# Both row parts of the dense u side in one matmul, with a VectorE add, in a hybrid decoder trunk

## Chip, cores and metric

The kernel runs on one core of one Trainium2 chip. The metric is the device time in microseconds (us) of one execution of the whole program; several executions are timed and the median is given. Further executions were recorded by the hardware profiler.

## The reference

One decoder layer for 256 tokens of width 1024: a mixer of two attention kinds with a residual, then a layer of retrieved experts (PEER) with a residual, then a last norm. Only the expert layer is touched:

```python
q = (hf @ wq).reshape(T, PEER_HEADS, 2, PEER_QDIM // 2)          # 256 tokens, 8 heads, 2 halves
s = jnp.einsum('thpd,hpnd->thpn', q, subkeys)                    # 128 keys for each half
s1, i1 = lax.top_k(s[:, :, 0], PEER_TOPK); s2, i2 = lax.top_k(s[:, :, 1], PEER_TOPK)   # 16 each
cand = s1[..., :, None] + s2[..., None, :]                       # 16 x 16 sums
top_s, pos = lax.top_k(cand, PEER_TOPK); idx = take_along_axis(cand_idx, pos)
w = jax.nn.softmax(top_s)
act = gelu(einsum('cd,chkd->chk', x_c, u[idx_c]))                # 16384 experts, rows of u
out = einsum('chk,chkd->cd', w_c * act, v[idx_c])                # rows of v
```

All data are float32.

## The kernel before

**Two ways for the experts.** 32 of the tokens (NG) read the rows of u and v that they chose: gathers by index bring 128 rows at a time to SBUF, VectorE takes 32 dot products with u rows (`dot`) and 32 weighted sums of v rows (`row_sum`). The other 224 tokens (TD) are computed against all 16384 experts: gelu(u·x) for every expert and token is made densely, multiplied by weights that one-hot matmuls spread over the experts, and multiplied with v.

**Two parts of each number.** A float32 product is made of rounded parts: `whi` is the weight rounded by ScalarE (`high`), `wlo` the rest, by VectorE (`low`); `ah` and `al` are the two parts of the tokens' rows. A block is one matrix of 128 experts by 1024. `block_t` runs 24 matmuls of 224 columns for it: ah with whi and al with whi in turn over 8 chunks, then ah with wlo, all into one region of PSUM.

**Stages.** Projections and attention; peer_wq (the queries, 16 blocks); u, first half (64 blocks, in pairs e = 0 to 31); u, second half (64 blocks), with the one-hot products beside it; v (128 blocks); and a tail that adds, transposes, norms and writes.

**Order.** `slot` issues one block: the load of a block two or three ahead (`fetch`, SyncE's queue, three raw buffers), then what stands in `first`, whi of the block two ahead, its wlo, what was put into `late`, what stands in `pre`, and last the block's matmuls. whi and wlo have three buffers each as well. In PSUM the names pj, pT, pS and pO have two banks each.

**Beside the matmuls of the first half** the top-16 search, the softmax and the look-up of the indices run. They are a list of steps, each with a price in us; `advance(us)` adds to a credit and runs the steps that it pays for. In the first half each slot adds PACE. The steps: 16 picks over rows of keys for each of the two token halves b (most on VectorE), `cands`, four picks `best`, `decode` (shifts and five casts), `soft_exp`, `choose`, then for both sets k = 0, 1: `look_idx`, `look_eq`, `look_tab`, `look_mul`, `look_sum` and `look_end` (four sums that halve a 128x2048 bf16 tile down to 128x128). `route` sends the 32 tokens' indices to memory and back as gather indices; `tables(b)` transposes weights and indices for the one-hot products. `tokens_out` lays the 32 tokens' rows out for the gathers by a GpSimd transfer.

A pair's end in the first half is one line, gelu read from PSUM by ScalarE (L1229):

```python
nc.scalar.activation(g, pu, AF.Gelu)
```

Of the kernel before, what the change touches and what calls it, by code (L numbers as in the profile page):

```python
# [141 lines left out]
def body(tc, nc, a):  # L142
# [849 lines left out]
    def decode(b):  # L992
        def it(name, dt=U32):
            return sel.tile([P, 8, 16], dt, name=name)
        pos = cp[b]
        hi4, lo4, hi2, lo2 = it("hi4"), it("lo4"), it("hi2"), it("lo2")
        nc.vector.tensor_scalar(hi4, pos, 4, None, OP.logical_shift_right)
        nc.vector.tensor_scalar(lo4, pos, 15, None, OP.bitwise_and)
        nc.vector.tensor_scalar(hi2, pos, 2, None, OP.logical_shift_right)
        nc.vector.tensor_scalar(lo2, pos, 3, None, OP.bitwise_and)  # L1000
        f = [it(f"f{k}", F32) for k in range(5)]
        for k, s in enumerate((hi4, lo4, hi2, lo2, pos)):
            nc.vector.tensor_copy(f[k], s)
        fs[b] = f
# [23 lines left out]
    def look_idx(b, k):  # L1028
        tib[b, k] = sel.tile([P, 8, 16], BF, name="tib", bufs=2)
        nc.vector.tensor_copy(tib[b, k], ti[b][:, :, k])  # L1030

# [11 lines left out]
    def look_sum(b, k):  # L1043
        e = eq[k]
        for n in (8, 4):
            nc.vector.tensor_tensor(e[:, :, 0:n], e[:, :, 0:n], e[:, :, n:2 * n], OP.add)
# [69 lines left out]
    for b in range(2):  # L1116
        steps.append((1.2, cands, b))
        for m in range(4):
            steps += pick(best, b, m)
            if b == 1 and m == 0:  # L1120
                steps.append((0.5, tables, 0))
        steps += [(0.3, soft_sub, b), (1.2, decode, b), (0.1, soft_exp, b), (1.2, choose, b), (0.2, look_idx, b, 0),
                  (1.15, look_eq, b, 0), (0.0, look_tab, b, 0), (0.7, soft_div, b), (0.2, look_idx, b, 1),
                  (1.15, look_mul, b, 0),
                  (1.15, look_eq, b, 1), (0.0, look_tab, b, 1), (0.95, look_sum, b, 0), (0.6, look_end, b, 0), (1.15, look_mul, b, 1),
                  (0.95, look_sum, b, 1), (0.6, look_end, b, 1)]
        if b == 0:
            steps.append((0.3, route))
    first_dot = next(k for k, v in enumerate(steps) if v[1:] == (soft_sub, 1))
    front, behind = steps[:first_dot], steps[first_dot:]  # L1130
    share, done, n = sum(v[0] for v in behind) / DOTS[0], 0.0, 0
    for v in behind:
        front.append(v)
        done += v[0]
        while n < DOTS[0] and done >= share * (n + 0.5):
            front.append((1.35, dot, n))
            n += 1
    steps = front + [(0.5, tables, 1)]
    credit = [0.0]
# [67 lines left out]
    def u_pair(e, first=((), ()), pre=((), ())):  # L1207
        box = []

        def use(hi, lo):  # L1210
# [20 lines left out]

        slot(use, first[0], pre[0])
        slot(use, first[1], pre[1])
        late.append(evac)

    for e in range(32):
        pre = ((rows_out,), (io_tables,)) if e == 0 else ((lambda: score(7),), ()) if e == 1 else ((), ())
        if e == 4:
# [152 lines left out]
    def fold_in():  # L1391
        nc.gpsimd.dma_start(xq[1].rearrange("p (g d) -> p g d", g=NR),
                            ys.rearrange("(g t) (c d) -> (t c) g d", t=NG, c=NR))

    def fold():
        n = D // 2
        while n >= D // NR:
            nc.gpsimd.tensor_tensor(xq[1][:, :n], xq[1][:, :n], xq[1][:, n:2 * n], OP.add)
# [40 lines left out]
    n += 3 + 5 * (NG - 1) // 2  # L1439
    at_slot(n + 2, "v", fold_in)  # L1440
# [31 lines left out]
    def turn_rows(c):  # L1472
        for b in range(2):
            nc.tensor.transpose(turned[c // 4 * 2 + b][:TB, (c % 4) * P:(c % 4 + 1) * P],
                                lasts[c][:, b * TB:(b + 1) * TB], ident)
# [7 lines left out]
    def total(b, c0, c1, n):  # L1483
        d = c0 // 4
        cs = slice((c0 - 4 * d) * P, (c1 - 4 * d) * P)
        nc.scalar.activation(whole[:, cs], turned[2 * d + b][:TB, cs], AF.Square, scale=1.0 / 32.0,
                             accum_out=sq[b][:, n:n + 1])
# [60 lines left out]
```

## Time and profile before

| what | value |
|---|---|
| median of 3 runs | 983.03 us (982.72 to 983.94) |
| profiled execution | 983.31 us; its span 981.5 us |
| busy in the span | TensorE 968.4, VectorE 801.7, ScalarE 587.7, GpSimd 141.2 us |
| u side, first half | 275.0 to 448.1 us |
| u side, second half | 448.1 to 646.7 us |
| v side | 646.7 to 957.3 us |

The span is the recorded stretch from first to last instruction; the execution's time has some 1.8 us more around it. PE is TensorE, PEld its weight loads, DVE VectorE, ACT ScalarE, POOL GpSimd, SP SyncE. A row of a group gives line, engine, operation, output and inputs, their shapes, the count, then busy time and mean duration in ns, then the engine's idle time before and what ended it. A row of the timeline gives start, duration and the instruction, in square brackets its engine's idle time before it and what ended that. A row of the windows gives start:end, length, busy time of each engine with its count of instructions, the granted clock of TensorE, the share of DMA time and GB/s. A row of the chain gives start, length, engine, output and line.

### The profile page before, as it was taken

The numbers are of one execution on the slowest core, as the hardware profiler recorded it, in microseconds if no ns is written. First come the engines' busy times: TensorE is split into PE (matmuls) and PEld (weight loads), VectorE is DVE, ScalarE is ACT, GpSimd is POOL, SyncE is SP. The second block draws the span as 40 slices with busy tenths as digits, with TensorE's granted clock in tenths as the row PEclk, the third lists the DMA queues.
The fourth block names the chain that finished last, engine by engine and source line by source line (L and its number), as shares of the span: only waits on it lengthen the run. The fifth ranks groups of instructions, "written<-read, shape, count | busy, mean of one in ns | idle before, by whom it ended". The sixth has DMA issues, their size and how long they took to land.

```text
span 981.5 us, 20223 instructions
## 1 busy us (share of the span) xinstructions
PE 968.4 (99%) x7825; PEld 938.0 (96%) x7825; DVE 801.7 (82%) x1486; ACT 587.7 (60%) x1073; POOL 141.2 (14%) x113
## 2 busy tenths in 40 slices
PE   9999999999999999999999999999999999999995
PEld 7898999999999999999999999999999999999995
DVE  5788876877889998887989999878778888888766
ACT  7545544656555665556988888655555555555563
POOL 3000110000000011321001001013313333333100
PEclk9999999999999999999999999999999999999999
DMA  8723434566556667887656655678878888787771
GB/s 274 264 90 111 124 114 132 173 195 188 176 174 219 220 200 253 309 277 265 204 194 198 211 183 183 215 262 291 294 271 299 296 287 293 287 293 292 274 224 44
DMA packets 61424, 217.24 MB, mean 221 GB/s; under 512 B 7120, under 2 KB 8320, under 8 KB 61320
## 3 DMA queue, kind: packets, MB, share of 16 engines
q1 hardware_dynamic: 48352, 174.42, 54.0%
q0 software_dynamic: 11280, 39.68, 11.0%
q10 hardware_dynamic: 1696, 1.84, 0.6%
q8 instruction: 62, 1.02, 0.4%
q14 instruction: 34, 0.28, 0.1%
HBM read 212.86 MB, written 2.52 MB: 219 GB/s over the span
## 4 chain that ended last, share of the span: by engine, by line
PE 91%; DVE 5%; ACT 1%; DMA 1%; issue 1%; SPq 0%; DVEq 0%; ACTq 0%
PE pj L372 50%; PE acc L1351 21%; PE acc L1355 11%; PE pw L1298 3%; DVE wlo L204 1%; PE pS L665 1%; PE pS L504 1%; PE pT L637 1%; PE pS L1166 1%; DMA xg<-in_x 1%; DMA raw<-in_w_t 1%; ACT whi L200 0%; PE pO L648 0%; PE pO L649 0%; PE pj L769 0%
## 5 line engine op out<-in xcount | busy, mean ns | idle before, releaser
L204 DVE TENSOR_TENSOR wlo<-raw,whi 128x1024 fp32r<-128x1024 f32 (+2 forms) x329 | 398.9, 1213 | 100.1 <-ACT whi L200 99.2
L200 ACT ACTIVATE whi<-raw 128x1024 fp32r<-128x1024 f32 (+2 forms) x329 | 343.7, 1045 | 138.1 <-PE pj L372 51.7
L372 PE MATMUL pj<-ah,whi 128*128 128x224 f32 (+1 forms) x1344 | 320.0, 282 | 0.2
L372 PE MATMUL pj<-al,whi 128*128 128x224 f32 (+1 forms) x1344 | 314.0, 276 | 0.6 <-DVE al L332 0.4
L372 PEld LDWEIGHTS pj<-al,whi 128*128 128x128 f32 x1344 | 257.5, 192 | 2.2 <-DVE al L332 1.0
L372 PEld LDWEIGHTS pj<-ah,whi 128*128 128x128 f32 x1344 | 256.7, 191 | 2.1 <-issue 1.2
L1351 PE MATMUL acc<-co,whi 128*128 128x448 f32 x1024 | 231.1, 367 | 0.1
L1351 PEld LDWEIGHTS acc<-co,whi 128*128 128x128 f32 x1024 | 182.8, 189 | 11.8 <-issue 0.3
L372 PE MATMUL pj<-ah,wlo 128*128 128x224 f32 (+1 forms) x1344 | 180.8, 276 | 0.0
L372 PEld LDWEIGHTS pj<-ah,wlo 128*128 128x128 f32 x1344 | 165.9, 191 | 0.0
L1355 PEld LDWEIGHTS acc<-co,wlo 128*128 128x128 f32 x1024 | 134.8, 191 | 4.2 <-DVE wlo L204 0.8
L1355 PE MATMUL acc<-co,wlo 128*128 128x224 f32 x1024 | 135.1, 273 | 0.5 <-DVE wlo L204 0.5
L1262 ACT ACTIVATE co<-G 128x224 fp32r<-128x224 f32 x128 | 50.1, 392 | 142.1 <-PE acc L1355 142.1
L1091 POOL DMA_INDIRECT row<-in_v_n,sidx x32 | 62.2, 1944 | 146.4 <-DVE ysum L1386 125.2
L1286 ACT ACTIVATE onehot<-onehot,wl 128x128 f16<-128x128 f16 x224 | 71.3, 392 | 6.3 <-DVE onehot L1290 5.9
L1263 DVE TENSOR_TENSOR co<-G,co 128x224 fp32r<-128x224 f32 x128 | 50.4, 394 | 22.2 <-ACT co L1262 21.9
L1091 POOL DMA_INDIRECT row<-in_u_n,sidx x19 | 32.8, 1729 | 218.0 <-DVE row L1101 217.4
L372 PE MATMUL pj<-bh,whi 128*128 128x256 f32 x192 | 48.0, 286 | 0.0
L372 PE MATMUL pj<-bl,whi 128*128 128x256 f32 x192 | 47.4, 284 | 0.0
L1386 DVE SCALAR_TENSOR_TENSOR ysum<-row,acts,ysum 128x1024 f32<-128x1024 f32 x31 | 39.7, 1280 | 0.0
L632 ACT ACTIVATE prob<-pS,nm 128x128 f32<-128x128 f32 (+1 forms) x48 | 19.8, 416 | 30.6 <-DVE nm L629 30.6
L372 PEld LDWEIGHTS pj<-bl,whi 128*128 128x128 f32 x192 | 36.5, 190 | 0.0
(323 smaller groups left out, 929.5 us busy)
## 6 DMA issues: line engine op xcount, KB each, us to landing
raw<-in_u_t SPq DMA_DIRECT2D x128, 512.0 KB, 3.5
raw<-in_v_n SPq DMA_DIRECT2D x128, 512.0 KB, 4.3
raw<-in_w_m SPq DMA_DIRECT2D x16, 512.0 KB, 3.5
raw<-in_w_q SPq DMA_DIRECT2D x16, 512.0 KB, 3.7
raw<-in_w_t SPq DMA_DIRECT2D x15, 512.0 KB, 5.0
raw<-in_w_b SPq DMA_DIRECT2D x8, 512.0 KB, 3.5
raw<-in_w_o SPq DMA_DIRECT2D x8, 512.0 KB, 3.6
sg<-in_w SPq DMA_DIRECT2D x4, 512.0 KB, 6.4
```

What stands on the lines that cost most here:

```text
L200: return [lambda s=slice(u, min(v, n)): nc.scalar.activation(hi[:, s], raws[k][:, s], AF.Copy) for u, v in cuts]
L204: nc.vector.tensor_tensor(lo[:, cs], raws[k][:, cs], hi[:, cs].bitcast(F32), OP.subtract)
L372: nc.tensor.matmul(out, (wl if v == 2 else wh)[:, c], (l if v == 1 else h)[:, c], start=(i == 0), stop=(i == len(seq) - 1))
L632: nc.scalar.activation(p[:, o], src[b], AF.Exp, bias=nm[:, b:b + 1], accum_out=sums[:, b, h:h + 1])
L1091: nc.gpsimd.indirect_dma_start(rows_of_step(n), None, src, bass.IndirectOffsetOnAxis(ap=sidx[:, n % NG:n % NG + 1], axis=0))
L1262: nc.scalar.activation(t[:, :TD], g, AF.Copy)
L1263: nc.vector.tensor_tensor(t[:, TD:], g, t[:, :TD].bitcast(F32), OP.subtract)
L1286: nc.scalar.activation(E[:, 1, t], E[:, 1, t], AF.Copy, scale=wl[:, n:n + 1])
L1298: nc.tensor.matmul(pw[:, t * P:(t + 1) * P], E[:, 0, t], E[:, 2 - s, t], start=(s == 0), stop=(s == 1))
L1351: nc.tensor.matmul(acc[c][:, :2 * TD], w[0][:, c * P:(c + 1) * P], coefs[k], start=(k == 0), stop=False, skip_group_check=True)
L1355: nc.tensor.matmul(acc[c][:, small], w[1][:, c * P:(c + 1) * P], coefs[k][:, :TD], start=False, stop=(k == P - 1), skip_group_check=True)
L1386: nc.vector.scalar_tensor_tensor(ysum, t, w, ysum, OP.mult, OP.add)
```

## The change

In the first 30 of the 32 pairs (WIDE), `use_both` takes the place of `block_t`: ah and al become two slices of one tile `both`, so that one matmul of 448 columns multiplies whi with both parts; al's product lands in the lower half's neighbour, and wlo with ah (224 columns) is added to that upper half. That is 8 matmuls of 448 columns and 8 of 224 a block, each block in a bank of its own (pj for a pair's first block, pT for its second). `evac_both` ends a pair: ScalarE copies the two upper halves to SBUF (`lowsum`), VectorE adds the lower ones one slot later, ScalarE takes the gelu in place a slot after that.

```diff
-PACE = 1.29
+PACE = 0.92
-DOTS = (13, 22)
-FETCH = 18
+DOTS = 12
+WIDE = 30
...
-    ah = hx.tile([P, NC, T], F32R, name="ah")
-    al = hx.tile([P, NC, T], F32R, name="al")
+    both = hx.tile([P, NC, 2, T], F32R, name="both")
+    ah, al = both[:, :, 0], both[:, :, 1]
...
+        def use_both(hi, lo):
+            o = bank("pT" if box else "pj")
+            box.append(o)
+            wh, wl = (v.rearrange("p (c m) -> p c m", m=P) for v in (hi, lo))
+            for c in range(NC):
+                nc.tensor.matmul(o[:, :2 * TD], wh[:, c], both[:, c, :, NG:], start=(c == 0), stop=False,
+                                 skip_group_check=True)
+            for c in range(NC):
+                nc.tensor.matmul(o[:, TD:2 * TD], wl[:, c], ah[:, c, NG:], start=False, stop=(c == NC - 1),
+                                 skip_group_check=True)
+
+        def evac_both():
+            g = G[e // 32][:, 2 * (e % 32):2 * (e % 32) + 2]
+            t = sel.tile([P, 2, TD], F32, name="lowsum", bufs=2)
+            for j in range(2):
+                nc.scalar.activation(t[:, j], box[j][:, TD:2 * TD], AF.Copy)
+            def add():
+                for j in range(2):
+                    nc.vector.tensor_tensor(g[:, j], t[:, j], box[j][:, :TD], OP.add)
+                late.append(lambda: nc.scalar.activation(g, g, AF.Gelu))
+            late.append(add)
+            spots["blocks"] += 2
```

The work beside it moves. The five casts of `decode` and the cast of `look_idx` go from VectorE to ScalarE, the four sums of each look-up set from VectorE to GpSimd. `route` and `tables(0)` come later in the list, `tables(1)` leaves it and stands at the last pair. The dots leave the first half (13 there before): 12 stand in the second half (before 9), 20 in the v side (before 10), and there dots and row sums stand every second block instead of every 2.5. The row buffers of the first half go, and one of the two loads of the 32 tokens' rows (`tokens_in`) with them.

```diff
         for k, s in enumerate((hi4, lo4, hi2, lo2, pos)):
-            nc.vector.tensor_copy(f[k], s)
+            nc.scalar.activation(f[k], s, AF.Copy)
...
         for n in (8, 4):
-            nc.vector.tensor_tensor(e[:, :, 0:n], e[:, :, 0:n], e[:, :, n:2 * n], OP.add)
+            nc.gpsimd.tensor_tensor(e[:, :, 0:n], e[:, :, 0:n], e[:, :, n:2 * n], OP.add)
...
+        if e == 31:
+            pre = (), (lambda: tables(1),)
...
     for k in range(2):
-        at_slot(3 + 2 * k, "pre", rows_in, DOTS[0] + k)
-    for n in range(*DOTS):
-        at_slot(9 + 6 * (n - DOTS[0]), "pre", dot, n)
+        at_slot(3 + 2 * k, "pre", rows_in, k)
+    for n in range(DOTS):
+        at_slot(9 + 9 * n // 2, "pre", dot, n)
...
-    for n in range(DOTS[1], NG):
-        at_slot(1 + 5 * (n - DOTS[1]) // 2, "v", dot, n)
+    for n in range(DOTS, NG):
+        at_slot(1 + 2 * (n - DOTS), "v", dot, n)
...
-        at_slot(n + 3 + 5 * k // 2, "v", row_sum, k)
+        at_slot(n + 3 + 2 * k, "v", row_sum, k)
```

Smaller edits: in peer_wq three pairs advance by 1.6 and 1.4 instead of 1.3 and 1.2; in the tail chunk 7's transposes get two banks of their own, and the last multiplication by the norm is split in two to follow that (384 and 128 columns).

VectorE, in the first half at blocks 4 and 5. Before (sc holds the scores, tv and ti the values and indices found; wlo_3690 is of block 6, wlo_3728 of block 7):

```order
L204 TENSOR_TENSOR wlo_3690<-raw_3641,whi_3689 128x1024 [waits DMAHW6_49,PE_49,Activation_49]
L947 MATCH_REPLACE sc_2783<-tv1_2806,sc_2783 128x128 [waits DVE_49] x2
L949 MAX tv1_2806<-sc_2783 128x8 [waits DVE_49] x2
L951 MAX_INDEX ti1_2808<-tv1_2806,sc_2783 128x8 [waits DVE_49] x2
L204 TENSOR_TENSOR wlo_3728<-raw_3677,whi_3727 128x1024 [waits DMAHW7_49,PE_49,Activation_49]
```

After, at the same place (wlo_3658 is of block 6, wlo_3689 of block 7, pj_3605 and pT_3632 the banks of pair 1):

```order
L204 TENSOR_TENSOR wlo_3658<-raw_3622,whi_3657 128x1024 [waits DMAHW6_49,PE_49,Activation_49]
L939 MAX tv1_2804<-sc_2782 128x8 x2
L941 MAX_INDEX ti1_2806<-tv1_2804,sc_2782 128x8 [waits DVE_49] x2
L204 TENSOR_TENSOR wlo_3689<-raw_3649,whi_3688 128x1024 [waits DMAHW7_49,PE_49,Activation_49]
L1221 TENSOR_TENSOR G0_2781<-lowsum_3662,pj_3605 128x224
L1221 TENSOR_TENSOR G0_2781<-lowsum_3662,pT_3632 128x224
```

The adds of pair 1 now stand behind wlo of block 7. On TensorE block 6 (pair 3) takes the banks that pair 1 had, and its first matmul carries a wait for VectorE:

```order
L1207 MATMUL pj_3727<-both_137,whi_3657 128x448 [waits DVE_49,PE_49,Activation_49]
L1207 MATMUL pj_3727<-both_137,whi_3657 128x448 x7
L1210 MATMUL pj_3727<-both_137,wlo_3658 128x224 x8
L1207 MATMUL pT_3756<-both_137,whi_3688 128x448 [waits DVE_49,Activation_49]
L1207 MATMUL pT_3756<-both_137,whi_3688 128x448 x7
L1210 MATMUL pT_3756<-both_137,wlo_3689 128x224 x8
```

In the order before, block 6's first matmul waits for ScalarE alone, and its rows alternate between ah and al.

ScalarE, at the second decode and softmax (f0 to f4 are the casts, wsm the weights). Before:

```order
L983 ACT_TABLE_LOAD [waits DMASW2_49]
L983 ACTIVATE wsm_5029<-wsm_5029 128x128 [waits DVE_49]
L200 ACTIVATE whi_5149<-raw_5110 128x1024 [waits DMAHW5_49,DVE_49,PE_49]
L200 ACTIVATE whi_5189<-raw_5144 128x1024 [waits DMAHW6_49,DVE_49,PE_49]
L1229 ACT_TABLE_LOAD
L1229 ACTIVATE G0_2782<-pj_5119 128x448 [waits PE_49]
L200 ACTIVATE whi_5225<-raw_5177 128x1024 [waits DMAHW7_49,DVE_49,PE_49]
```

After (lowsum is the copy of the upper halves):

```order
L1001 ACTIVATE f3_5143<-lo2_5135 128x128 [waits DVE_49]
L1001 ACTIVATE f4_5144<-cp1_2810 128x128
L981 ACT_TABLE_LOAD
L981 ACTIVATE wsm_5105<-wsm_5105 128x128 [waits DMASW1_49]
L200 ACTIVATE whi_5151<-raw_5097 128x1024 [waits DMAHW6_49,PE_49,Activation_49]
L1222 ACT_TABLE_LOAD
L1222 ACTIVATE G0_2781<-G0_2781 128x448
L1217 ACTIVATE lowsum_5156<-pj_5080 128x224
L1217 ACTIVATE lowsum_5156<-pT_5113 128x224 [waits PE_49]
L200 ACTIVATE whi_5188<-raw_5130 128x1024 [waits DMAHW7_49,PE_49,Activation_49]
```

Casts and copies have joined the exp and the two table loads, and the copies stand behind the second load.

GpSimd, at the first look-up, where before the queue held only transfers there (sc is the tile that is summed, idx the result):

```order
L1079 DMA xhs_2793<-xhd_2794 4x2x16384 [waits DMASW5_49]
L1044 TENSOR_TENSOR sc_2782<-sc_2782 128x8x128 [waits DVE_49,PE_49]
L1044 TENSOR_TENSOR sc_2782<-sc_2782 128x8x64 [waits Pool_49]
L1049 TENSOR_TENSOR sc_2782<-sc_2782 128x8x32 [waits Pool_49]
L1050 TENSOR_TENSOR idx_4702<-sc_2782 128x128 [waits Pool_49]
```

These four rows stood on VectorE between wlo of two blocks, and the transfer of `tokens_out` (xhs) stands ahead of them as before.

More of the change, by code (lines that the diff above doesn't have):

```diff
@@ L934, in body @@
     xrow = flat(xt[:, 4:8])[:NG]
-    xq = [sel.tile([P, D], F32, name="xq")]
-    rows_at = [flat(xt[:, 0:4]), xhw, g_wide]
-    rows_wide = []
+    xq, rows_wide = [], []
     def top16_a(*sets):
@@ L1029, in look_idx @@
         tib[b, k] = sel.tile([P, 8, 16], BF, name="tib", bufs=2)
-        nc.vector.tensor_copy(tib[b, k], ti[b][:, :, k])
+        nc.scalar.activation(tib[b, k], ti[b][:, :, k], AF.Copy)
     def look_tab(b, k):
@@ L1050, in look_end @@
         o = ii[b, k] = sel.tile([P, 8, 16], F32, name="idx", bufs=2)
-        nc.vector.tensor_tensor(e[:, :, 0:2], e[:, :, 0:2], e[:, :, 2:4], OP.add)
-        nc.vector.tensor_tensor(o, e[:, :, 0], e[:, :, 1], OP.add)
+        nc.gpsimd.tensor_tensor(e[:, :, 0:2], e[:, :, 0:2], e[:, :, 2:4], OP.add)
+        nc.gpsimd.tensor_tensor(o, e[:, :, 0], e[:, :, 1], OP.add)
     def tables(b):
@@ L1086, in rows_of_step @@
     def rows_of_step(n):
-        return rows_at[n % 3] if n < DOTS[0] else rows_wide[n % 2]
+        return rows_wide[n % 2]
     def rows_in(n):
@@ L1094, in rows_next @@
     def rows_next(n):
-        m = n + (3 if n < DOTS[0] else 2)
-        if m < (DOTS[0] if n < DOTS[0] else 2 * NG):
-            rows_in(m)
+        if n + 2 < 2 * NG:
+            rows_in(n + 2)
     def dot(n):
@@ L1119, in body @@
             steps += pick(best, b, m)
-            if b == 1 and m == 0:
-                steps.append((0.5, tables, 0))
-        steps += [(0.3, soft_sub, b), (1.2, decode, b), (0.1, soft_exp, b), (1.2, choose, b), (0.2, look_idx, b, 0),
+            if b == 1 and m == 2:
+                steps += [(0.3, route), (0.5, tables, 0)]
+        steps += [(0.3, soft_sub, b), (0.9, decode, b), (0.1, soft_exp, b), (1.2, choose, b), (0.2, look_idx, b, 0),
                   (1.15, look_eq, b, 0), (0.0, look_tab, b, 0), (0.7, soft_div, b), (0.2, look_idx, b, 1),
                   (1.15, look_mul, b, 0),
[L1125 to L1138, printed above, removed]
+                  (1.15, look_eq, b, 1), (0.0, look_tab, b, 1), (0.05, look_sum, b, 0), (0.05, look_end, b, 0), (1.15, look_mul, b, 1),
+                  (0.05, look_sum, b, 1), (0.05, look_end, b, 1)]
     credit = [0.0]
@@ L1197, in body @@
             if m > 1:
-                first.append(lambda: advance(1.3 if m < 7 else 1.0))
-                second.append(lambda: advance(0.6 if m in (2, 7) else 1.2))
+                first.append(lambda m=m: advance(1.6 if 2 < m < 6 else 1.3 if m < 7 else 1.0))
+                second.append(lambda: advance(0.6 if m in (2, 7) else 1.4 if m < 6 else 1.2))
         pair(q_evac(m), bh, bl, ((begin_norm,) if m == 1 else (), ()), (first, second), last=(6, 7) if m == 0 else (), to=late)
@@ L1230, in evac @@
             spots["blocks"] += 2
-        slot(use, first[0], pre[0])
-        slot(use, first[1], pre[1])
-        late.append(evac)
+        f = use_both if e < WIDE else use
+        slot(f, first[0], pre[0])
+        slot(f, first[1], pre[1])
+        late.append(evac_both if e < WIDE else evac)
     for e in range(32):
@@ L1397, in fold @@
         while n >= D // NR:
-            nc.gpsimd.tensor_tensor(xq[1][:, :n], xq[1][:, :n], xq[1][:, n:2 * n], OP.add)
+            nc.gpsimd.tensor_tensor(xq[0][:, :n], xq[0][:, :n], xq[0][:, n:2 * n], OP.add)
             n //= 2
-        nc.gpsimd.dma_start(yd.rearrange("t (c d) -> (t c) d", c=NR), xq[1][:, :D // NR])
-    gf = xq[1]
+        nc.gpsimd.dma_start(yd.rearrange("t (c d) -> (t c) d", c=NR), xq[0][:, :D // NR])
+    gf = xq[0]
     few = [r[:NG] for r in rows_wide]
@@ L1457, in body @@
     assert not jobs, jobs
-    turned = [acc[0], acc[1], acc[2], acc[3]]
+    turned = acc[0:6]
     lasts = {}
@@ L1473, in turn_rows @@
         for b in range(2):
-            nc.tensor.transpose(turned[c // 4 * 2 + b][:TB, (c % 4) * P:(c % 4 + 1) * P],
+            k, o = (4, 0) if c == 7 else (c // 4 * 2, c % 4 * P)
+            nc.tensor.transpose(turned[k + b][:TB, o:o + P],
                                 lasts[c][:, b * TB:(b + 1) * TB], ident)
```

21 lines of the change are left out of this document (9 added, 12 removed).

## Prediction

> **What bounds the kernel now.** I read the page first, then the four stages as windows, then the chain of work that ended last.
>
> ```profile
> PE 968.4 (99%) x7825; PEld 938.0 (96%) x7825; DVE 801.7 (82%) x1486; ACT 587.7 (60%) x1073; POOL 141.2 (14%) x113
> PE 91%; DVE 5%; ACT 1%; DMA 1%; issue 1%; SPq 0%; DVEq 0%; ACTq 0%
> 281.25:448.07 166.82, 166.82 (x1497) 166.82 (x1496) 149.60 (x430) 94.23 (x115) 22.14 (x21) 1.00 0.73 242
> 448.07:646.70 198.63, 198.63 (x1988) 197.86 (x1987) 173.97 (x225) 157.43 (x376) 16.40 (x11) 1.00 0.60 205
> 646.70:957.30 310.60, 310.60 (x1976) 296.12 (x1976) 243.98 (x304) 169.48 (x256) 84.49 (x48) 1.00 0.81 284
> 370.26 75.04 PE pj L372 x672
> 649.21 1.63 PE acc L1351 x8
> 651.72 1.63 PE acc L1351 x8
> ```
>
> Page: TensorE is busy 99% of the span and carries 91% of the chain. Windows (length; busy PE, PE loads, VectorE, ScalarE, GpSimd; granted clock; DMA share; GB/s): in the first half of the u side (first row) TensorE never waits, at full clock; VectorE is next with 149.60 of 166.82 us, 90%. So time is won by shorter TensorE work, and lost where another engine makes it wait. The chain rows price the work: 672 matmuls are 28 blocks of 24, so a block of the u side takes 75.04/28 = 2.680 us. The v side already does both parts in one matmul; its blocks start 651.72 − 649.21 = 2.51 us apart.
>
> **The wide matmuls.** A block becomes 8 matmuls of 448 columns and 8 of 224, the v side's very mix. With its 2.51 us, 30 pairs win 60 × 0.167 = 10.0 us. Bounds: 0 (nothing won) to 60 × 0.17. I take the v side's value, since operand shapes and count are the same.
>
> **The new wait.** Before, a pair's bank is read by one ScalarE gelu. Now ScalarE copies the upper halves, VectorE adds them to the lower ones, and TensorE's first matmul of pair e+2 waits for the add of pair e (the order shows that wait). The add stands in VectorE's row behind wlo of block 2e+5, and that wlo reuses the buffer of block 2e+2, so it cannot start before block 2e+3 does.
>
> ```profile
> L204 DVE TENSOR_TENSOR wlo<-raw,whi 128x1024 fp32r<-128x1024 f32 x65 | 79.0, 1215 | 16.6 <-ACT whi L200 16.4
> L200 ACT ACTIVATE whi<-raw 128x1024 fp32r<-128x1024 f32 x64 | 67.9, 1060 | 72.2 <-DMA raw<-in_u_t 48.1 <-PE pj L372 15.8 <-DVE xhw L1101 2.1
> L1263 DVE TENSOR_TENSOR co<-G,co 128x224 fp32r<-128x224 f32 x128 | 50.4, 394 | 22.2 <-ACT co L1262 21.9
> 283.10 1.19 DVE L204 TENSOR_TENSOR wlo<-raw,whi 128x1024 fp32r<-128x1024 f32 x1
> 284.22 0.47 DVE L941 MAX8 tv<-sc 128x8 f32<-128x128 f32 x2
> ```
>
> wlo takes 1.22 us, and the next instruction starts 1.12 us after it (283.10 to 284.22); an add of 224 elements is nearest to co, 0.39, so 0.31 of VectorE's time. (Bounds of the add: 0.3, and 0.7 for twice the work if reading PSUM is slow.) The whi that block 2e+5 needs may be written when block 2e+2 is through its eight wide matmuls, 1.63 us after its start by the v rows; it takes 1.06, so it is there 0.2 us after block 2e+3 starts. wlo 1.12 and the add 0.39 bring 1.8 of 2.51 us with the hand-overs. TensorE's slack against VectorE is thus about 0.7 us. Before, a wlo may come nearly two blocks late at no cost, since whi and wlo have three buffers each. Behind the add on VectorE wait the look-up and top-16 steps, which nothing waits for at once, and on ScalarE the gelu, which nothing reads before the second half. On the mean the work fits: per pair 2 × 1.12 + 2 × 0.31 + about 2 us of steps (PACE grants 1.84 by the code's own prices) make 4.9 of 5.03 us. The casts, sums and 13 dots taken away pay for the 60 adds. But every local lateness beyond 0.7 us is now TensorE's. Small ones when the stage starts: 0.5 us, bounds 0 to 1.5.
>
> **First lateness: one blocked transfer.** Before the change:
>
> ```profile
> 275.00 0.35 PE L372 MATMUL pj<-ah,whi 128*128 128x224 f32 x1
> 281.25 0.35 PE L372 MATMUL pj<-ah,whi 128*128 128x224 f32 x1
> 282.91 0.61 POOL L1081 DMA_DIRECT2D xhs<-xhd  x1 [1.92 <-DMA xhd<-xhw]
> DMA to landing us min/median/max: 8.9/8.9/8.9
> 292.99 1.06 ACT L200 ACTIVATE whi<-raw 128x1024 fp32r<-128x1024 f32 x1 [5.50 <-DMA raw<-in_u_t]
> 294.08 1.23 DVE L204 TENSOR_TENSOR wlo<-raw,whi 128x1024 fp32r<-128x1024 f32 x1 [2.83 <-ACT whi L200]
> ```
>
> The stage's first matmul stands at 275.00, block 2 starts at 281.25 (two blocks and 0.9 us of other matmuls later), so block 5 at 289.3. GpSimd's broadcast xhs (issued 282.91, 8.9 us to landing, at 291.8) holds up the load of raw for block 7; ScalarE waits 5.50 us for it, VectorE makes wlo of block 7 at 294.08, 4.8 us after block 5 began. TensorE did not notice, since block 7 itself starts only at 289.3 + 2 × 2.68 = 294.7. The broadcast stays where it is. Now the add of pair 1 stands behind that wlo: 294.08 + 1.23 + 0.39 + 0.2 = 295.9, while block 6 is due at 275.0 + 0.9 + 6 × 2.51 = 291.0. Stall: 4.9 us (bounds 0, if the load slips past the broadcast, and 6).
>
> **Second: the table loads of ScalarE.**
>
> ```profile
> 338.66 1.28 ACT L983 ACT_TABLE_LOAD   x1
> 339.96 0.31 ACT L983 ACTIVATE wsm<-wsm 128x128 f32<-128x128 f32 x1
> 340.18 1.05 ACT L200 ACTIVATE whi<-raw 128x1024 fp32r<-128x1024 f32 x1
> 341.24 1.28 ACT L1229 ACT_TABLE_LOAD   x1
> 342.53 0.55 ACT L1229 ACTIVATE G<-pj 128x448 f32<-128x448 f32 x1
> 342.98 1.05 ACT L200 ACTIVATE whi<-raw 128x1024 fp32r<-128x1024 f32 x1
> L1034 ACT ACTIVATE sc<-tib 128x1024 bf16<-128x1024 bf16 x8 | 8.0, 1044 | 1.1 <-DVE sc L1041 0.9 <-DVE tib L1030 0.2
> ```
>
> Today exp, with a table load on either side, costs TensorE nothing. After, ScalarE's order at the second decode is five casts (5 × 0.22, the spacing of the 128x128 exp), load 1.30, exp 0.22, whi 1.06, load 1.29, gelu 0.45, two copies of half its width 0.3 each, whi 0.97: 7.0 us. With wlo 1.12 and add 0.39 behind it on VectorE that is 8.5, against two blocks, 5.03: 3.4 us (block 54). At the first decode the order parts the pieces differently: 1.3, 1.0 and 0.1 at blocks 32, 34 and 36. Two more ScalarE pieces in odd blocks: look_tab (1.04 each) 0.95, and tables(0), moved, 0.55. Sum 7.3; bounds 1 (the chain starts early enough) to 9.
>
> **Third: sums on GpSimd.**
>
> ```profile
> L1046 DVE TENSOR_TENSOR sc<-sc 128x1024 bf16<-128x1024 bf16 (+1 forms) x8 | 4.4, 555 | 0.1
> 101.53 1.22 DVE L204 TENSOR_TENSOR wlo<-raw,whi 128x1024 fp32r<-128x1024 f32 x1
> 101.75 2.12 POOL L682 TENSOR_TENSOR y<-y,ytmp 128x512 f32<-128x512 f32 x1 [1.87 <-DVE ytmp L681]
> L1398 POOL TENSOR_TENSOR xq<-xq 128x256 f32<-128x256 f32 x1 | 0.8, 768 | 0.1
> 927.09 1.23 DVE L204 TENSOR_TENSOR wlo<-raw,whi 128x1024 fp32r<-128x1024 f32 x1 [0.56 <-ACT whi L200]
> 927.35 2.97 POOL L1398 TENSOR_TENSOR xq<-xq 128x512 f32<-128x512 f32 x2 [4.77 <-DMA xq<-ys]
> 928.65 1.07 DVE L1263 TENSOR_TENSOR co<-G,co 128x224 fp32r<-128x224 f32 x1 [0.34 <-ACT co L1262]
> 929.64 1.76 DVE L204 TENSOR_TENSOR wlo<-raw,whi 128x1024 fp32r<-128x1024 f32 x1
> 931.32 0.38 DVE L1263 TENSOR_TENSOR co<-G,co 128x224 fp32r<-128x224 f32 x1
> ```
>
> At 101.75 GpSimd's sum takes 2.12 us, and 0.9 of it is the rest of VectorE's wlo: alone it is some 1.25. At 928.65, while GpSimd sums, VectorE's co takes 1.07 instead of 0.38 and the next wlo 1.76 instead of 1.23. Each holds the other off while both read two tensors of SBUF. By width (1.25 for 512, 0.77 for 256) a set of four sums (1024, 512, 256, 128) is 2.5 + 1.28 + 0.77 + 0.4 = 4.95 us; four sets, 19.8. Against it VectorE is rid of the first sums (555 ns each) and two smaller ones a set. wlo and the look steps all read two SBUF tensors, the adds read PSUM and are not held. Going down the order with these durations, blocks 38, 40, 42 stall 1.6, 1.9 and 3.2 us, blocks 60 and 62 2.5 and 1.1, and tables(1), which waits for the last sum, takes 0.6: 11.0 (rounded). As a control: of 4.95 a set, 0.7 is slack and some 1.6 are adds and waits for whi anyway, so 2.6 × 4 = 10.6. Bounds 0 (bf16 sums far quicker) and 13.
>
> [...]
>
> **What else moves.**
>
> ```profile
> L1386 DVE SCALAR_TENSOR_TENSOR ysum<-row,acts,ysum 128x1024 f32<-128x1024 f32 x31 | 39.7, 1280 | 0.0
> row<-in_v_n,sidx POOLq DMA_INDIRECT x32, 6.4
> PE acc L1474 <- ACT row L1486: 0.9, 2, 0.6
> ```
>
> Dots in the second half go from 9 to 12: 3 × 1.28 = 3.8 us on a VectorE with 198.63 − 173.97 = 24.7 free; covered, 0 (to 1). The v side takes 20 dots instead of 10 and fits 32 row sums closer: 12.8 us on 66.6 free. A gather then has 1.3 + 6.4 = 7.7 us of the four blocks, 10.05, that two row buffers leave: slack 2.3, DMA share 0.81 to about 0.87; 0 (to 2). GpSimd's queue loses the first half's gathers, of which none stood ahead of a wait; the two now issued at blocks 3 and 5 of the second half have over 10 us to the first dot, at block 9. The rows' step (route) is moved past two of four picks on VectorE and its transfers past GpSimd's sums; nothing waits for them before those gathers: 0. The earlier steps in the peer_wq stage load VectorE by under 1 us: 0. The tail's own banks may take some of the 0.9 us wait: 0, bounds ±0.3.
>
> **Sum.** 983.31 (the profiled execution, 0.28 above the median) − 10.0 + 0.5 + 4.9 + 7.3 + 11.0 = 997.0; against the median, 996.7, forecast 996.5.
>
> **Rivals.** First, the other side: the lateness is absorbed, as today. If the wait for a bank left as much room as the three wlo buffers do today (4.8 us at block 7 cost nothing), the stalls vanish and 983.3 − 10.0 = 973.3 follows, up to 981 with some left. It decides from a tolerance of 2 us instead of 0.7: each stall loses 1.3 and none falls below 0, and 3.6 + 2.1 + 0.3 + 0.6 + 1.9 + 1.2 = 9.7 are left, less than the 10.0 won. For it: today's record of a TensorE that never waits. Against: the order has TensorE wait on VectorE at every even block.
>
> Second: the sums are cheap. If GpSimd's bf16 sums hold VectorE little, the third term is 0 to 6 and the time 986 to 990; without the blocked transfer too, 981 to 985.
>
> Third: the v side's gathers land late. Beyond 8.6 us instead of 6.4, each further us costs up to 1 us in each of some 30 gathers: over 1003. Against: DMA share 0.81 with 6.4 us.
>
> Fourth: the wide matmuls into one bank are no quicker here; blocks stay at 2.68 and the time is about 1006. Against: the v rows.
>
> **Chances.** All three stalls 0.48 (own range 991 to 1003); cheap sums 0.18 (983 to 991); absorbed 0.27 (971 to 981); late gathers 0.05; no quicker 0.02. Under 0.2%, some 2 us, a measurement of this kernel cannot tell from no change. Faster by more: 0.27 + 0.01 = 0.28. Within: 0.07, of the second case. Slower: 0.65. The range 974 to 1003 holds all but 0.06 of the absorbed case, 0.02 of the first and the last two: 0.85.
>
> **What would show it.** Right: blocks 2.51 apart; TensorE idle in even blocks of the first half, released by VectorE's add of G (L1221); such waits of 4 to 5 us at block 6, 2 to 4 around both decodes, and at blocks 38 to 42 and 60 to 62 where GpSimd's L1044 runs 2.5 us and wlo exceeds 1.22; first half 461 instead of 448 at its end. Wrong: no such waits (absorbed), L1044 near 1 us (cheap sums), DVE dot or sum waiting for row in the v side (late gathers).

## The result, and the profile after

The changed kernel takes 995.21 us (median of 4, 992.14 to 996.66) against 983.0 us: ratio 1.0114, interval 1.0101 to 1.0127. The forecast was 996.5, slower. The sum came out within 2 us, but a term that was too large and one that was missing cancelled.

The page of the changed kernel (busy time; the chain), then its windows (start:end, length, busy PE, PE loads, VectorE, ScalarE, GpSimd, granted clock, DMA share, GB/s):

```profile
PE 966.0 (97%) x7345; PEld 926.1 (93%) x7345; DVE 820.8 (83%) x1518; ACT 607.0 (61%) x1147; POOL 174.8 (18%) x128
PE 53%; DVE 1%; ACT 0%; issue 0%; DVEq 0%; ACTq 0%
300.00:360.00 60.00, 60.00 (x382) 56.93 (x381) 57.49 (x206) 35.86 (x59) 0.00 (x0) 1.00 0.62 205
372.00:400.00 28.00, 23.92 (x151) 22.33 (x150) 27.20 (x44) 16.32 (x26) 13.63 (x8) 1.00 0.51 174
461.00:659.50 198.50, 198.50 (x1987) 197.87 (x1987) 176.38 (x230) 157.90 (x376) 20.28 (x13) 1.00 0.60 209
```

From 300 to 360 us TensorE never waits, at VectorE 57.49 of 60: the adds do fit beside the top-16 search. From 372 to 400, the first look-up, TensorE is busy 23.92 of 28 while VectorE is busy 27.20. The second half of the u side is as long as before (198.5 against 198.63). The program now reaches the second half at 461.0 instead of 448.1, 12.9 us later; of that 0.8 us come back behind the start of the v side (span 993.5 − 659.5 = 334.0, before 981.5 − 646.7 = 334.8), all of it in the tail: from the end of the v side's last matmul to the end of the span it is 9.7 us, before 10.5.

The timeline of TensorE in the first half, all its waits to block 58, with the neighbours of the two longest (one more, 0.36 us, stands at block 62):

```profile
295.15 2.73 PE L1207 MATMUL pj<-both,whi 128*128 128x448 f32 x8 [3.68 <-DVE G L1221]
297.68 1.82 PE L1210 MATMUL pj<-both,wlo 128*128 128x224 f32 x8
299.33 1.80 PE L1207 MATMUL pT<-both,whi 128*128 128x448 f32 x8
301.85 1.80 PE L1207 MATMUL pj<-both,whi 128*128 128x448 f32 x8
...
364.00 1.87 PE L1207 MATMUL pj<-both,whi 128*128 128x448 f32 x8 [1.24 <-ACT wsm L981]
370.10 1.87 PE L1207 MATMUL pj<-both,whi 128*128 128x448 f32 x8 [0.83 <-DVE G L1221]
381.86 1.87 PE L1207 MATMUL pj<-both,whi 128*128 128x448 f32 x8 [1.43 <-DVE G L1221]
388.08 1.87 PE L1207 MATMUL pj<-both,whi 128*128 128x448 f32 x8 [0.95 <-DVE G L1221]
395.05 1.86 PE L1207 MATMUL pj<-both,whi 128*128 128x448 f32 x8 [1.70 <-DVE G L1221]
416.18 1.87 PE L1207 MATMUL pj<-both,whi 128*128 128x448 f32 x8 [0.39 <-ACT whi L200]
429.93 3.33 PE L1207 MATMUL pj<-both,whi 128*128 128x448 f32 x8 [3.43 <-DVE G L1221]
434.73 2.30 PE L1207 MATMUL pT<-both,whi 128*128 128x448 f32 x8
437.75 1.80 PE L1207 MATMUL pj<-both,whi 128*128 128x448 f32 x8
444.28 1.87 PE L1207 MATMUL pj<-both,whi 128*128 128x448 f32 x8 [1.31 <-DVE G L1221]
```

Undisturbed blocks start 2.52 us apart (299.33 to 301.85), so the wide matmuls do save their 0.16 us each, 9.6 us over 60. The rows with a wait are blocks 6, 32, 34, 38, 40, 42, 50, 54 and 58, even blocks all. Two of them name ScalarE, but in the trace all ten waits, that of block 62 too, end 0.15 us after VectorE's add of the lower halves of two pairs earlier. Where TensorE does not wait, at the blocks from 8 to 30, that add is in time by 0.0 to 0.6 us. A second loss stands behind the two longest: block 6 takes 4.18 us (295.15 to 299.33), blocks 54 and 55 take 4.80 and 3.02. That is 1.7 and 2.8 us more than 2.52 with no wait in them. The windows show why: the granted clock is at 0.50.

```profile
296.00:299.00 3.00, 3.00 (x13) 2.79 (x12) 2.79 (x13) 1.44 (x3) 0.00 (x0) 0.50 0.46 164
429.93:433.00 3.07, 3.07 (x8) 2.77 (x9) 2.42 (x3) 2.89 (x5) 0.00 (x0) 0.50 0.72 212
```

The hold-ups between VectorE and GpSimd stand in their timelines:

```profile
378.20 4.23 POOL L1044 TENSOR_TENSOR sc<-sc 128x1024 bf16<-128x1024 bf16 x2 [94.54 <-DVE sc L1039]
378.20 3.21 DVE L204 TENSOR_TENSOR wlo<-raw,whi 128x1024 fp32r<-128x1024 f32 x1 [0.16 <-ACT whi L200]
381.34 0.37 DVE L1221 TENSOR_TENSOR G<-lowsum,pj 128x224 f32<-128x224 f32 x1
388.15 2.56 DVE L204 TENSOR_TENSOR wlo<-raw,whi 128x1024 fp32r<-128x1024 f32 x1
L1044 POOL TENSOR_TENSOR sc<-sc 128x1024 bf16<-128x1024 bf16 x4 | 10.3, 2582 | 124.5 <-DVE sc L1039 124.5
```

wlo, 1.2 us elsewhere, takes 3.21 and 2.56 while GpSimd sums; the add, which reads PSUM, keeps its 0.37. A first sum takes 2.58 us on the mean, but of two kinds: 2.14 and 2.15 where VectorE's wlo had to wait for it, 2.99 and 3.06 where it stood behind a wlo.

### The profile page after: what moved, and what is told of

It reads as the page before. It is cut to its first block, busy times and chain, and to the rows that moved or that the text cites. A ratio compares the mean times of both kernels' runs of the same rounds, so it can differ in the third digit from the quotient of the medians.

```text
span 993.5 us, 19455 instructions
## 1 busy us (share of the span) xinstructions
PE 966.0 (97%) x7345; PEld 926.1 (93%) x7345; DVE 820.8 (83%) x1518; ACT 607.0 (61%) x1147; POOL 174.8 (18%) x128
## 3 DMA queue, kind: packets, MB, share of 16 engines
HBM read 212.34 MB, written 2.52 MB: 216 GB/s over the span
## 4 chain that ended last, share of the span: by engine, by line
PE 53%; DVE 1%; ACT 0%; issue 0%; DVEq 0%; ACTq 0%
PE acc L1359 21%; PE pj L372 18%; PE acc L1363 11%; PE pw L1306 3%; DVE wlo L204 0%; ACT whi L200 0%; PE pj L1207 0%; PE pT L1207 0%; DVE raw L1539 0%; PE acc L1483 0%; DVE last L1478 0%; DVE x L1477 0%; PE pj L1210 0%; PE pT L1210 0%; ACT row L1494 0%
## 5 line engine op out<-in xcount | busy, mean ns | idle before, releaser
L204 DVE TENSOR_TENSOR wlo<-raw,whi 128x1024 fp32r<-128x1024 f32 (+2 forms) x329 | 406.7, 1237 | 98.5 <-ACT whi L200 94.9
L372 PE MATMUL pj<-both,whi 128*128 128x224 f32 (+1 forms) x1728 | 223.1, 281 | 0.9 <-ACT whi L200 0.4
L372 PEld LDWEIGHTS pj<-both,whi 128*128 128x128 f32 x1728 | 206.8, 191 | 4.3 <-issue 2.1
L372 PE MATMUL pj<-both,wlo 128*128 128x224 f32 (+1 forms) x864 | 117.2, 278 | 0.0
L372 PEld LDWEIGHTS pj<-both,wlo 128*128 128x128 f32 x864 | 107.5, 191 | 0.0
L1089 POOL DMA_INDIRECT row<-in_u_n,sidx x32 | 57.5, 1798 | 237.2 <-DVE row L1098 236.6
L1207 PE MATMUL pj<-both,whi 128*128 128x448 f32 x240 | 57.4, 383 | 15.0 <-DVE G L1221 13.3
L1207 PEld LDWEIGHTS pj<-both,whi 128*128 128x128 f32 x240 | 44.5, 195 | 19.5 <-ACT whi L200 12.1
L1207 PE MATMUL pT<-both,whi 128*128 128x448 f32 x240 | 54.6, 370 | 0.0
L1207 PEld LDWEIGHTS pT<-both,whi 128*128 128x128 f32 x240 | 43.5, 192 | 2.9
L1044 POOL TENSOR_TENSOR sc<-sc 128x1024 bf16<-128x1024 bf16 (+1 forms) x8 | 18.4, 2301 | 124.8 <-DVE sc L1039 124.5
```

The source lines that it names most:

```text
L204: nc.vector.tensor_tensor(lo[:, cs], raws[k][:, cs], hi[:, cs].bitcast(F32), OP.subtract)
L372: nc.tensor.matmul(out, (wl if v == 2 else wh)[:, c], (l if v == 1 else h)[:, c], start=(i == 0), stop=(i == len(seq) - 1))
L1044: nc.gpsimd.tensor_tensor(e[:, :, 0:n], e[:, :, 0:n], e[:, :, n:2 * n], OP.add)
L1089: nc.gpsimd.indirect_dma_start(rows_of_step(n), None, src, bass.IndirectOffsetOnAxis(ap=sidx[:, n % NG:n % NG + 1], axis=0))
L1207: nc.tensor.matmul(o[:, :2 * TD], wh[:, c], both[:, c, :, NG:], start=(c == 0), stop=False, skip_group_check=True)
```

## The experiments

All ratios are against the kernel before, measured on the same chip (983.5 us, in the last pair 984.2). Differences from the changed kernel are from its 995.21 us, which was taken beside a kernel before of 983.0 and has runs 4.5 us apart: they are good to about 2 us, and the profiles carry the finer claims.

### Narrow matmuls, all else changed

```diff
-WIDE = 30
+WIDE = 0
```

> The changed kernel with WIDE = 0: all 32 pairs of the first half by block_t and one gelu from PSUM, everything that moved stays moved. Theory (wide matmuls win 10 us, the wait of the bank on VectorE's add loses 22): without wide matmuls there is no such wait, blocks take 2.68 us, TensorE never waits for VectorE in the first half, and the time is 982 to 985, though GpSimd's sums and the blocked transfer are all still there. Rival (the moved work costs the time by itself, through GpSimd's sums or the later dots): 988 to 996.

Measured: 986.74 us, 1.0032 (1.0019 to 1.0044), between the two forecasts. TensorE no longer waits for any add, so the new wait is the cause of most of the loss: with wide matmuls the same program takes 8.5 us more, though they save 9.6. But 3 us remain that the expectation had at nothing. Its timeline of TensorE at the end of the first half:

```profile
448.01 0.47 PE L1055 MATMUL pO<-ident,idx 128*128 128x128 f32 x1 [2.05 <-POOL idx L1050]
448.14 3.50 PE L372 MATMUL pj<-both,whi 128*128 128x224 f32 x16
```

The transpose in tables(1) waits 2.05 us for GpSimd's last sum, and the next 16 matmuls take 3.50 us instead of 2.0: the granted clock is 0.50 from 447.8 to 451.2 us.

### The add one block earlier

```diff
-            late.append(add)
+            add()
```

> The changed kernel with VectorE's add one block earlier: behind wlo of block 2e+4, right after ScalarE's copies, instead of behind wlo of block 2e+5. Theory (only the tolerance of 0.7 us was short): it grows by a block, 2.5 us, to some 3.2; the stalls at blocks 32, 34, 38, 40, 42 and 58 vanish, block 54 keeps under 1 us, the blocked transfer, which then hits the add of pair 2 behind wlo of block 8, some 1 us; with no idle time over 3 us the granted clock stays at 1.0. Time 973 to 978, faster than before. Rival (the work does not fit on the mean, VectorE at 95 to 98%): the stalls come back elsewhere and the time is 985 or more. Second rival (the copies on ScalarE now hold VectorE): waits of VectorE for lowsum of about 0.5 us a pair, 980 to 988.

Measured: 986.86 us, 1.0045 (1.0026 to 1.0064). The add early wins some 8 us over the changed kernel, so tolerance was short; it does not win all. At blocks 12 to 32 the add is now in time by 0.7 to 2.5 us. The waits at blocks 32, 34, 38 and 58 are gone, others stay or move (blocks 8, 36, 40, 42, 44, 54 and 60: 9.0 us in all). The expectation that the clock stays at 1.0 without idle time over 3 us failed: the 2.37 us at block 60 lost it (0.51 from 439.4 to 441.5 us). The 3 us were an estimate; the changed kernel had lost its clock behind 3.43 and 3.68 us and kept it behind 1.70. The second rival falls: in the first half VectorE never waits for ScalarE's copies of the upper halves, only for whi. The first rival is right in one stretch only:

```profile
300.00:366.00 66.00, 66.00 (x419) 62.61 (x418) 62.47 (x221) 43.81 (x74) 0.00 (x0) 1.00 0.63 210
366.00:397.00 31.00, 27.18 (x170) 25.27 (x169) 30.00 (x46) 20.92 (x34) 14.70 (x8) 1.00 0.52 178
```

In the look-up VectorE is busy 30.0 of 31 us, its waits for GpSimd counted in: over a stretch that is full, a longer lead is used up. In the top-16 stretch there is no wait.

### The broadcast moved to the second half

```diff
-        if e == 4:
-            pre = (tokens_out,), ()
...
-    at_slot(1, "pre", tokens_in)
+    at_slot(0, "pre", tokens_out)
+    at_slot(4, "pre", tokens_in)
```

> The changed kernel with the broadcast of the 32 tokens' rows (tokens_out) moved from block 8 of the issue order in the first half to the first block of the second half, and its second leg (tokens_in) from block 1 to block 4 there. Theory (the broadcast delays the load of block 7 and so the add of pair 1): block 6 no longer waits 3.7 us, and the 1.7 us that blocks 6 lost to a lower granted clock behind that wait go too; time 5 to 6 us less than the changed kernel, 989 to 991. Rival (the load of block 7 is late for another reason, such as three raw buffers): the wait stays, 994 to 997.

Measured: 989.76 us, 1.0064 (1.0048 to 1.0081), 5.5 us less than the changed kernel. Block 6 now waits 0.46 instead of 3.68 us and keeps its clock, with 1.87 us for its eight wide matmuls instead of 2.73:

```profile
292.09 1.87 PE L1207 MATMUL pj<-both,whi 128*128 128x448 f32 x8 [0.46 <-DVE G L1221]
```

### Without the table loads

```diff
-        nc.scalar.activation(wsm[b], wsm[b], AF.Exp)
+        nc.scalar.activation(wsm[b], wsm[b], AF.Copy)
```

> The changed kernel with the exp of the softmax left out (a copy on ScalarE in its place, which needs no table load): what is computed changes, the work beside it does not. Theory (casts, two table loads, gelu and copies form one chain on ScalarE ahead of the add): 2.6 us less at each decode; the waits at blocks 32 and 54 go from 1.2 and 3.4 to 0 and about 1, the 2.8 us of lower clock behind the wait at block 54 vanish; 5 to 8 us less than the changed kernel, 987 to 990. Rival (VectorE is late at these blocks by its own work, decode and choose): the waits stay, 994 to 997.

Measured: 989.84 us, 1.007 (1.0054 to 1.0087), 5.4 us less.

```profile
363.45 1.86 PE L1207 MATMUL pj<-both,whi 128*128 128x448 f32 x8 [1.24 <-DVE G L1221]
426.05 1.87 PE L1207 MATMUL pj<-both,whi 128*128 128x448 f32 x8 [1.17 <-DVE G L1221]
```

Block 54 waits 1.17 instead of 3.43 us, as forecast, and its 2.8 us of low clock are gone; so is the 0.83 at block 34. Waits of 0.52 and 1.26 at blocks 56 and 60 stand in place of the 1.31 at block 58. Block 32 still waits 1.24: there the expectation failed. In the changed kernel the loads come only after the whi that this add needs; what stands ahead of that whi on ScalarE are the five casts and their wait of 1.30 us for VectorE's shifts (the last experiments take the casts away).

### The sums back on VectorE

```diff
-            nc.gpsimd.tensor_tensor(e[:, :, 0:n], ...
+            nc.vector.tensor_tensor(e[:, :, 0:n], ...
```

(and the two in look_end)

> The changed kernel with the four sums of each look-up set back on VectorE, at the place in the order and with the prices they have now. Theory (GpSimd's sums and VectorE hold each other off): wlo beside the look-up goes back to 1.2 us from up to 3.2; the waits at blocks 38, 40, 42 and 58, 6.1 us, give way to VectorE's own sums, 1.7 us a set, of which 0.7 is slack: some 4 us; 991 to 994. Rival (the waits there come from the look-up steps themselves, whatever adds): the waits stay and VectorE's load grows by 6.7 us: 997 to 1001.

Measured: 994.4 us, 1.0113 (1.0098 to 1.0129), no gain that counts, and neither forecast. Every wlo beside the look-up takes 1.2 us again, and the waits at blocks 38, 42 and 58 vanish. But with prices of 0.05 both sets run, each in one go, ahead of one pair's add, and a wait of 3.08 us grows at block 40:

```profile
388.98 3.08 PE L1207 MATMUL pj<-both,whi 128*128 128x448 f32 x8 [3.08 <-DVE G L1221]
```

The clock falls with it (block 40 takes 4.16 us). So this run shows that the hold-ups made the waits at blocks 38 and 58; at block 42 the longer wait just before may have given VectorE the time. It does not show that the sums are better off on VectorE.

### Matmuls put into the two long waits

```diff
+            if e in (3, 27) and len(box) == 1:
+                d = bank("pO")
+                for c in range(12):
+                    nc.tensor.matmul(d[:, :2 * TD], wh[:, c % NC], both[:, c % NC, :, NG:], start=True, stop=True)
```

> The changed kernel with 12 more matmuls of 448 columns into an unused bank ahead of blocks 6 and 54, which run in the time in which TensorE waits there anyway (12 x 0.2 = 2.5 of 3.7 and 3.4 us). Theory (the lower granted clock behind the two long waits, 1.7 and 2.8 us, comes from the idle time itself): the idle time left is about 1.2 and 1.0, the clock stays at 1.0, blocks 6, 54 and 55 take 2.5 to 2.6 us again; 4 to 4.5 less than the changed kernel, 990 to 992. Rival (the clock falls for another reason): same time, 994 to 997.

Measured: 992.47 us (991.21 to 995.67), 1.0097 (1.0076 to 1.0117). The median is 0.5 above the forecast, and one execution lies in the rival's range; the profile, of an execution of 991.42 us, shows what was asked:

```profile
290.59 2.62 PE L1209 MATMUL pO<-both,whi 128*128 128x448 f32 x12
294.68 1.87 PE L1211 MATMUL pj<-both,whi 128*128 128x448 f32 x8 [1.47 <-DVE G L1225]
297.27 1.80 PE L1211 MATMUL pT<-both,whi 128*128 128x448 f32 x8
```

Block 6 still has to wait for its add, but takes 2.59 us (294.68 to 297.27) instead of 4.18; block 54 waits 0.97 and takes 2.59 too. So here the low clock came from the idle time: with 1.47 and 0.97 us of it instead of 3.68 and 3.43, the rest filled with useless work, it is gone. Part of the gain goes again in waits of 0.52 and 1.27 at blocks 56 and 60, in place of 1.31 at block 58.

### Early add and moved broadcast

> The changed kernel with the add one block earlier and the broadcast moved, the sums still on GpSimd. Theory (the hold-ups between GpSimd and VectorE are what the early add could not absorb): the 1.7 us at block 7 go, the waits at blocks 35 to 43, 53 and 60 (8 to 9 us) stay: 984 to 986, and the combined kernel, whose sums are on VectorE, is some 8 to 10 us faster than this one. Rival (it was the blocked transfer that made all of VectorE late): 975 to 979, about the same as the combined kernel.

Measured: 983.93 us, 1.0008 (0.9996 to 1.0019): the loss is gone, no gain yet. The waits at blocks 36 to 44 and 54 are those of the early add alone to within 0.3 us, so the blocked transfer was not behind them. The transpose in tables(1) waits 2.48 us for GpSimd's last sum.

### All four together

The two edits above, the sums on VectorE, their prices 0.95 and 0.6 again, PACE 1.01.

> The changed kernel with four edits at once: the add one block earlier, the broadcast moved to the second half, the look-up sums back on VectorE at their old prices (0.95 and 0.6), and PACE 1.01 for the 5.8 us that the steps grow by. Theory (three causes, each of them taken away; VectorE's load without the hold-ups about 156 of 162 us): waits of 0 to 3 us in all remain in the first half, the granted clock stays at 1.0, and the 9.5 us of the wide matmuls show: 973 to 977, faster than before. Rival (VectorE is too full for the adds): the waits move into the top-16 stretch and 980 to 986 follows.

Measured: 980.03 us, 0.9963 (0.9951 to 0.9975): faster than before, and 3.9 us faster than with the sums on GpSimd, where 8 to 10 had been forecast; short of its own forecast by 3. The number lies in the rival's range, but in the long top-16 stretch ahead of block 32 TensorE does not wait. What its TensorE waits for (us in total, times, longest), the window of its look-up, and from the timelines block 32 and VectorE ahead of it:

```profile
PE pj L1207 <- DVE G L1221: 5.3, 5, 1.9
370.00:395.00 25.00, 25.00 (x160) 23.75 (x159) 24.86 (x70) 16.12 (x26) 0.00 (x0) 1.00 0.69 222
358.24 1.87 PE L1207 MATMUL pj<-both,whi 128*128 128x448 f32 x8 [1.90 <-DVE G L1221]
353.53 1.23 DVE L204 TENSOR_TENSOR wlo<-raw,whi 128x1024 fp32r<-128x1024 f32 x1 [3.33 <-ACT whi L200]
```

From 370 to 395 TensorE no longer waits, with VectorE at 24.86 of 25 us. The 5.3 us that are left lie at blocks 32, 36, 52, 54 and 58, around the decodes and behind the second one. At the first VectorE sits idle for 3.33 us for a whi, behind ScalarE's casts and table load. With the sums on GpSimd and PACE at 0.92 block 32 did not wait: the other PACE puts the decode elsewhere among the blocks.

### The casts back as well, and the exp later

```diff
-            nc.scalar.activation(f[k], s, AF.Copy)
+            nc.vector.tensor_copy(f[k], s)
```

and in the second kernel soft_exp behind choose.

> The combined kernel with the five casts of each decode back on VectorE as well (decode priced 1.2, PACE 1.02). Theory (ScalarE's chain of casts, table load, exp and whi keeps VectorE waiting 3.3 us at the first decode): the chain is 1.1 us shorter at each decode and VectorE has the time for the casts in its own wait; the waits at blocks 32 and 52 to 54, 1.9 and 2.0 us, fall to about 0.8 and 1; 2 us less than the combined kernel, 977 to 979. Rival (VectorE too full): the same or 1 us more, 980 to 982.

> The same as the kernel with the casts on VectorE, and the exp with its two table loads one step later, behind choose instead of behind decode. Theory (the chain is long because whi waits for what stands ahead of it on ScalarE): the loads then meet a ScalarE without casts and a VectorE with wlo of the next block done; waits around the decodes under 1 us each, 975 to 978. Rival (two loads and an exp, 2.8 us, hold a whi wherever they stand): no gain over the kernel with the casts on VectorE, within 1 us of it.

Measured: 977.64 us, 0.9932 (0.9919 to 0.9945), and 977.73 us, 0.9935 (0.9922 to 0.9947). With the casts on VectorE the wait at block 32 is gone altogether: the table load starts right behind the copies instead of 3.3 us after them, 2.2 of which ScalarE had waited for VectorE's shifts and 1.1 cast. So the casts and the wait that they bring are its cause, and the kernel is 2.4 us faster than the combined one (3 by the ratios). The second decode did not follow: TensorE still waits 1.08 and 1.91 us there. The exp one step later changes nothing in the median, its rival's forecast: at this second place, too, waits are left, 0.76, 1.47 and 0.65 us at blocks 36, 54 and 58. These two are the fastest kernels of the study.

## Why the prediction was right, and where not

The wide matmuls, put at 10.0: right (9.6), 2.52 us a block. The new wait, with a tolerance of 0.7 us: right, and if anything generous, since undisturbed adds are in time by 0.6 us at most. Every wait of the first half stands in an even block and ends 0.15 us after an add, and moving the add by one block is worth some 8 us. So the absorbing rival fell.

The blocked transfer, put at 4.9: the wait is 3.68, and the broadcast is its cause (moved, 0.46 is left). wlo of block 7 came at 293.48, 0.6 us sooner than in the profile before, and block 6 was due some 0.5 later than I had it:

```profile
293.48 1.23 DVE L204 TENSOR_TENSOR wlo<-raw,whi 128x1024 fp32r<-128x1024 f32 x1 [3.65 <-ACT whi L200]
```

ScalarE's chain, put at 7.3: the waits at blocks 32, 34, 50 and 54 are 1.24 + 0.83 + 0.39 + 3.43 = 5.9. At block 54 the loads are shown to be the main part, as forecast, and 1.24 and 0.83 at blocks 32 and 34 are near the 1.3 and 1.0 of the sum. What is short is the 0.95 for look_tab, of which no wait shows. That the loads lie behind block 32 was an error of the later expectation, not of this step.

GpSimd's sums, put at 11.0: 1.43 + 0.95 + 1.70 at blocks 38, 40 and 42 (forecast 1.6, 1.9, 3.2) and 1.31 at block 58 in place of 4.2 at blocks 60, 62 and the tables; 5.4 in all. The mechanism was right. The price was not: a set took 6.9 us on the mean (2.58 + 2.02 + 1.40 + 0.91), not 4.95, because VectorE also holds GpSimd off, while a first sum that was not held took 2.14, not 2.5. Mis-sized above all was how much of it TensorE pays: the last set ran from 450.7 us on, beside the blocks of the two narrow pairs, where only the adds of pair 29 are still waited for (0.36 us at block 62).

The low clock, not in the sum at all: 4.5 us behind blocks 6 and 54. Together the first half lost 12.9 + 9.6 = 22.5 us: 15.0 of waits to block 58, 4.5 of low clock, the other 3 at block 62, in some 0.15 us around each wait and in small delays. I had 23.7. That the total came so close is luck: the sums were 5.6 too dear, ScalarE and the transfer 2.6, and against that stood the clock, which I did not have, and the small delays, of which I had 0.5. The step that failed is the size of the third term, and the missing one.

What else moves, put at 0: the second half and the gathers cost TensorE nothing, as forecast; from the v side's first matmul to its last it is 324.5 us in both kernels. But the gathers did lose their slack of 2.3 us. In the v side VectorE waits for rows six times, which it never did before:

```profile
DVE row L1098 <- DMA row<-in_u_n,sidx: 1.5, 4, 0.6
DVE ysum L1394 <- DMA row<-in_v_n,sidx: 0.7, 2, 0.4
```

That was the named sign of late gathers; with 0.6 us at most, on an engine with time to spare, it cost nothing. The wait of tables(1) for GpSimd, put at 0.6 us, costs 2.05 us in the narrow kernel and 2.48 with early add and moved broadcast, where less else is late. The tail, put at 0 to 0.3, gave 0.8 back: the 0.9 us that its matmuls waited for ScalarE's row are gone, while their waits for VectorE's last grew from 0.3 to 0.7. No run takes the tail's edits apart.

## What to carry to other kernels

An evacuation that needs a second engine gives that engine a deadline: count the time from the last thing it queues behind to the moment the bank is needed, not its mean load. If that slack is under a block (here 0.6 us at most), look for the place one block earlier before anything else (here worth some 8 us). Work moved off a busy engine is priced by what it blocks where it lands: an engine that it holds off (here a wlo of 1.2 us took up to 3.21 beside GpSimd's sums), or one whose next instruction someone waits for.

## What the runs showed of the hardware

In these traces TensorE's granted clock fell to 0.50 around a wait, and always for the same time: each such stretch of the first half lasted 3.41 us, two of them twice that (behind block 54 of the changed kernel and block 6 of the one with the sums on VectorE). What was lost, 1.5 to 2.9 us, is about half of what TensorE worked in the stretch, and did not grow with the wait: 1.91 us cost as much as 3.91.

Nor did the length of the wait alone decide. Waits of 3.0 us and more always did it (7 in four kernels); waits of up to 1.7 us never did. In between, the same wait of 2.37 us at block 60 once lost the clock (the early add) and once did not (with the broadcast moved too), nor did 2.48 us at tables(1) of that kernel:

```profile
439.45 3.65 PE L372 MATMUL pj<-both,whi 128*128 128x224 f32 x16 [2.37 <-DVE G L1221]
436.18 2.02 PE L372 MATMUL pj<-both,whi 128*128 128x224 f32 x16 [2.37 <-DVE G L1221]
447.14 0.33 PE L1055 MATMUL pO<-ident,idx 128*128 128x128 f32 x1 [2.48 <-POOL idx L1050]
415.85 2.97 PE L1207 MATMUL pj<-both,whi 128*128 128x448 f32 x8 [1.91 <-DVE G L1221]
```

The traces show what did. The starts of the low stretches of one run lie whole multiples of 3.413 us apart (changed kernel: 428.98 − 295.86 = 39 × 3.413; sums on VectorE: 28 and 12 times). So the time of a run can be cut into cells of 3.413 us, with a boundary where a low stretch starts, and a wait falls on them as it may. The clock also fell at the end of the runs, in the changed kernel at 988.77 us, 164 cells after 428.98, and in the one before at 976.78, which gives the cells of those without a fall inside. Counted by cells, the first halves of all twelve profiles have no exception: each of the ten cells in which TensorE stood idle for 1.86 us or more was followed by half the clock, and no cell with 1.83 or less was. The 2.37 us that lost it lie in one cell; the 2.37 that did not are 1.83 in one and 0.54 in the next, the 2.48 are 1.20 and 1.28. The 1.91 us (last row, block 54 with the casts on VectorE: 2.97 us for eight wide matmuls that take 1.80) lie in one cell; 1.90 us at block 32 of the combined kernel are split and lost nothing. A cell at half clock with 0.64 or 0.95 us idle was followed by a second one, those with less than 0.3 by full clock. The limit between 1.83 and 1.86 us is read from these runs alone.

The changed kernel's runs lie 4.5 us apart (992.14 to 996.66), those of before 1.2; the fastest has a mean granted clock of 0.996, the three others 0.992. Clocks lost in one run and kept in another would do that, which is argued: only one execution has a trace.

GpSimd and VectorE held each other off for whole instructions where both read two tensors of SBUF: a sum of 128 elements took 0.43 us while VectorE stood idle and 1.29 beside a wlo, a wlo up to 3.21 instead of 1.2, of which 1.08 came after the end of the sum beside it (380.33 us). The adds, which read one of their two inputs from PSUM, took 0.37 beside the sums and 0.38 elsewhere. The profile counts this waiting as busy time: the 30.0 of 31 us above are in part such waits.
